# The output weight of an attention layer, split into halves earlier and kept in DRAM

## The chip, the cores and the metric

The kernel runs on one core of one Trainium2 chip. The core has a matrix engine (TensorE, PE in the profile; PEld is its weight load), three engines for element-wise work (VectorE, DVE; ScalarE, ACT; GpSimd, POOL) and SyncE (SP), which issues most of the DMA transfers. Each engine works through its own instructions in order and waits on semaphores for the others. The metric is the device time of one execution in microseconds. In the profile, TensorE's clock is the share of full speed that was granted to it.

## The reference, cut to what matters

One inference step of a small decoder: a Mamba-2 (SSD) layer, then a latent attention (MLA) layer, then a norm. There are two groups of tokens, a prompt of 1024 tokens and a sample of 8 sequences with 8 new tokens each and a paged cache of 2048 tokens. All is float32. Of the MLA layer this matters here:

```python
gate = proj[..., o3:]                                   # 1024 columns of w_in
s = (einsum('bqhc,bkc->bhqk', q_lat, ckv)               # 16 heads, latent of 256
     + einsum('bqhr,bkr->bhqk', q_pe, kpe)) * MLA_SCALE # rotary key of 32
p = exp(s - max(s)); acc = einsum('bhqk,bkc->bhqc', p, ckv); l = sum(p)
o = einsum('bhqc,chv->bqhv', acc / l, w_uv)
out = einsum('bte,ed->btd', o * silu(gate), w_out)      # w_out is 1024 x 1024
h = h + out                                             # then rms_norm(h, final_norm_w)
```

The sample's `ckv` and `kpe` come page by page from a pool through `page_table`, and partial results are merged with running maxima. The prompt is causal over itself.

## The kernel before

**Halves.** A matmul operand is kept as two rounded halves: `hi` is the value rounded to the matrix engine's input type and `lo` is the rest. A product is then three matmuls (hi x hi, hi x lo, lo x hi). `split` (lines 128 to 131) makes the halves: ScalarE copies `hi`, VectorE subtracts for `lo`. Every weight goes through a raw tile and a split before use (`load_w`, line 269 on).

**The stages of the MLA layer.** (1) `mla_in` (L1432): norm of the SSD layer's output, then eight gate blocks. `gate_block` (L1409) loads 128 columns of the gate's weight, splits them into tiles of tag `wg` (three buffers each for `hi` and `lo`), runs 72 matmuls (three groups of 24: 8 slices of the model dimension by three products), and ScalarE writes silu of each group into `gt`, which SP stores to DRAM (`g_d`). Between the blocks, `gather_kpe` (L1952) fetches the sample's rotary keys, transposes and splits them and stores the halves in DRAM (`kpe_d`). (2) The projections of keys, values and queries. (3) `mla_heads` (L1896): 16 heads of the prompt, 12 steps each. In a step `qk` (L1824) makes scores for 128 keys by 512 queries (`st`), ScalarE takes the exponential twice (`th` rounded, `P` full), POOL or VectorE subtracts for the rest `tl`, and three steps later (`LEAD`) `pv` (L1851) multiplies by the values. The row maxima come in as two further rows of the operand (rows 96 and 97): `maxpass` computes them one head ahead, and small DMAs (`kTh<-nr`, L1822) write them into the query operand. When a half of a head is done, its closing (L1881) multiplies by the softmax's denominator and the gate on POOL, and stores to DRAM (`og_d`). Key operands sit in four tiles `kT[0..3]`, query operands in three `qT`; head 15 takes `kT[0]` as its query tile (`q_of`, L1630). (4) The sample's pages: `flow` (L2225) runs over 32 items of 512 cached tokens. Item n's step transposes page n + 1 (`turn`, `ct` to `cTh`, `cTl`), transposes the weights of page n - 1 (`turn_p`, `pt`), makes scores (`scores`, tiles `sc4`, with the rotary key `tk` as the last product), takes the softmax (`weigh`, which gives `P`), fetches a later page, multiplies by the values of page n - 1 (`values`) and splits the raw page n + 1 (`halves`). Each sequence has four items; its new tokens add `first_scores`, `first_values` and `first_acc` at the first item, and `turn_acc` transposes the finished sum. The first eleven units of this flow (`FLOW`) run inside head 15. (5) `MlaOut.pieces` (L2327): for each of the 8 prompt tiles of 128 rows and the sample's rows, the gated output is read back from `og_d`, split into `oh`, `ol` and multiplied by the halves of the output weight `w5h`, `w5l`, in the order of `WORD`. `next(out.fill)` in the flow puts half of a tile's product into each page's step, from n = 4 on.

**The passage.** Between the last head's last product and the first pieces of the output (n = 2 to 5 of the flow) the tiles of the heads are freed and those of the output are opened over them.

**The weight before.** Two of eight raw slices of the output weight are loaded in `preload` at the beginning of head 15 (L2018), three more when the heads' tiles are free (L2274) and the last three as raw buffers get free (`weight`, L2309). `weight_split` (L2314) is called in the flow at n = 2 (four slices), 3 (two) and 4 (two): `hi` on ScalarE, `lo` in quarters on POOL for every second slice and on VectorE for the others.

**The rotary keys before.** `load_tk` (L2054) reads the halves of two pages, as plain numbers, into a staging tile `tkr` by three DMAs of 128 KB, and `round_tk` (L2061) copies each page on POOL into the operand `tk`.

**Who sets the order.** In the heads and the sample, TensorE's and GpSimd's instructions stay in the order in which the program writes them (`manual_schedule`). ScalarE, VectorE and SP are ordered by a planner that simulates a timeline; so their order can change where the program's text does not.

```python
            if len(closing) and closing[0][0] <= 12 * h + t:
                closing.pop(0)[1]()
            if len(held) > LEAD:
                c = hd.pv(*held.pop(0))
                if c:
                    closing.append((12 * h + t + 2, c))
```

## Time and profile before

| what | value |
|---|---|
| time, median of 3 | 1967.74 us (1966.07 to 1968.34) |
| the profiled execution | 1968.61 us, span 1966.8 us |
| TensorE busy | 1890.8 us, 96% |
| VectorE, ScalarE, GpSimd busy | 1185.9, 1108.1, 833.7 us |
| DMA moved | 207.02 MB, mean 105 GB/s |
| mean granted clock of TensorE | 0.984 |

The span runs from the first to the last instruction of the profiled execution; the time of that execution is 1.8 us longer. By the windows of the trace, the SSD layer lasts to about 1050 us of the span, the gates run from 1060 to 1168, the projections to 1340, the heads from 1340 to 1690, the passage from 1690 to 1734, pages and pieces to about 1930. A wait such as `PE pt L2174 <- ACT P L2089` reads: TensorE stood before the instruction of line 2174 that writes `pt`, and what ended the wait was ScalarE's instruction of line 2089 that writes `P`.

### The profile page before, as it was taken

What the parts mean: (1) busy time and instruction counts of PE and PEld (TensorE: products, weight loads), DVE (VectorE), ACT (ScalarE), POOL (GpSimd) and SP (SyncE); (2) the same over time, 40 slices, a digit from 0 to 9 for tenths busy, and PEclk for the clock granted to TensorE, in tenths of its full rate; (3) what the DMA queues carried; (4) which work ended last, traced back from release to release, by engine and by line L of the source; (5) the groups of instructions that cost most, each with busy time, mean ns of one, the idle gap of its engine ahead of it and who ended that gap; (6) DMA issues with size and microseconds to landing.
All of it is one profiled execution on the core that took longest, in us unless ns stands there. A gap on an engine that the chain in (4) does not pass through costs nothing.

```text
span 1966.8 us, 33784 instructions
## 1 busy us (share of the span) xinstructions
PE 1890.8 (96%) x11953; PEld 1735.2 (88%) x11953; DVE 1185.9 (60%) x2562; ACT 1108.1 (56%) x2605; POOL 833.7 (42%) x1138
## 2 busy tenths in 40 slices
PE   7999999999999999799999999999999999799998
PEld 6999999999999999687787998998888888678887
DVE  5457575757575757544425214566777776666665
ACT  5556666666666666653334324435777777655552
POOL 2037373737363657233000001104554556866661
PEclk9999999999999999899999999999999999899999
DMA  5213233333333332544544442222121113554451
GB/s 151 53 55 96 84 96 86 94 91 90 93 88 92 91 89 82 204 153 157 189 177 137 132 160 69 77 104 74 56 55 43 51 43 98 161 161 147 144 151 38
DMA packets 182545, 207.02 MB, mean 105 GB/s; under 512 B 19004, under 2 KB 147912, under 8 KB 181992
## 3 DMA queue, kind: packets, MB, share of 16 engines
q1 hardware_dynamic: 177544, 185.85, 31.2%
q0 software_dynamic: 4752, 18.88, 2.9%
q8 instruction: 95, 1.56, 0.3%
q14 instruction: 74, 0.61, 0.1%
q10 hardware_dynamic: 80, 0.13, 0.0%
HBM read 151.50 MB, written 53.15 MB: 104 GB/s over the span
## 4 chain that ended last, share of the span: by engine, by line
PE 77%; POOL 7%; issue 4%; DMA 4%; DVE 4%; ACT 3%; SPq 1%; POOLq 0%; DVEq 0%; ACTq 0%
PE pj L89 23%; PE pj L101 9%; PE pq L101 6%; PE pob L101 4%; PE poa L101 4%; POOL kvl L2147 3%; PE py L865 3%; PE sc L1801 2%; PE st L1834 2%; PE st L1835 2%; PE st L1836 2%; PE o L1867 2%; PE o L1866 1%; PE o L1865 1%; PE pk L101 1%
## 5 line engine op out<-in xcount | busy, mean ns | idle before, releaser
L89 PE MATMUL pj<-xh,wih 128*128 128x384 f32 (+1 forms) x768 | 255.7, 333 | 0.0
L89 PE MATMUL pj<-xh,wil 128*128 128x384 f32 (+1 forms) x768 | 251.2, 327 | 0.0
L89 PE MATMUL pj<-xl,wih 128*128 128x384 f32 (+1 forms) x768 | 251.0, 327 | 0.0
L1848 POOL TENSOR_TENSOR tl<-P,th 128x384 fp32r<-128x384 f32 (+1 forms) x144 | 132.9, 928 | 135.6 <-ACT P L1846 74.7
L131 DVE TENSOR_TENSOR wil<-wraw,wih 128x512 fp32r<-128x512 f32 x92 | 70.4, 765 | 173.8 <-ACT wih L130 173.8
L902 POOL TENSOR_TENSOR y<-y,xD 128x256 f32<-128x256 f32 x64 | 83.9, 1312 | 149.3 <-DVE y L901 138.5
L89 PEld LDWEIGHTS pj<-xh,wih 128*128 128x128 f32 x768 | 145.0, 189 | 0.2
L89 PEld LDWEIGHTS pj<-xl,wih 128*128 128x128 f32 x768 | 144.8, 189 | 0.3
L89 PEld LDWEIGHTS pj<-xh,wil 128*128 128x128 f32 x768 | 144.6, 188 | 0.0
L101 PE MATMUL pj<-wih,xh 128*128 128x256 f32 x504 | 143.3, 288 | 0.0
L101 PE MATMUL pj<-wil,xh 128*128 128x256 f32 (+1 forms) x504 | 139.2, 282 | 0.0
L1845 ACT ACTIVATE th<-st 128x512 fp32r<-128x512 f32 x192 | 94.4, 492 | 68.3 <-PE st L1841 46.6
L497 DVE SCALAR_TENSOR_TENSOR acc<-raw,vec,acc 128x1112 f32<-128x1112 f32 x84 | 130.5, 1554 | 0.2
L101 PE MATMUL pj<-wih,xl 128*128 128x256 f32 x448 | 126.6, 283 | 0.0
L2147 POOL TENSOR_TENSOR kvl<-pgr,kvh 128x256 fp32r<-128x256 f32 x128 | 98.7, 798 | 53.7 <-ACT kvh L2145 53.7
L131 POOL TENSOR_TENSOR xddl<-xdd,xddh 128x256 fp32r<-128x256 f32 x64 | 63.2, 987 | 119.5 <-ACT xddh L130 119.5
L130 ACT CAST Ch<-acc 128x128 fp32r<-128x128 f32 x56 | 16.9, 301 | 152.8 <-PE py L89 152.8
L101 PEld LDWEIGHTS pj<-wih,xh 128*128 128x128 f32 x504 | 96.0, 191 | 0.0
L1846 ACT ACTIVATE P<-st 128x512 f32<-128x512 f32 x192 | 93.4, 486 | 2.7 <-DVE tl L1848 2.1
L101 PEld LDWEIGHTS pj<-wil,xh 128*128 128x128 f32 (+1 forms) x504 | 93.0, 185 | 0.6
L840 ACT ACTIVATE M<-M,tok 128x128 f32<-128x128 f32 (+1 forms) x288 | 90.5, 388 | 1.8 <-DMA M<-acs_d 1.8
L101 PEld LDWEIGHTS pj<-wih,xl 128*128 128x128 f32 x448 | 85.5, 191 | 0.0
(981 smaller groups left out, 6276.0 us busy)
## 6 DMA issues: line engine op xcount, KB each, us to landing
wraw<-in_ssd_w_in SPq DMA_DIRECT2D x92, 256.0 KB
M<-acs_d SPq DMA_DIRECT2D x64, 256.0 KB
y_d<-xD SPq DMA_DIRECT2D x64, 128.0 KB
s<-in_state_ssm SPq DMA_DIRECT2D x32, 256.0 KB
out_s_ssm<-s SPq DMA_DIRECT2D x32, 256.0 KB
wraw<-in_ssd_w_out SPq DMA_DIRECT2D x16, 512.0 KB
q_d<-qt SPq DMA_DIRECT2D x32, 192.0 KB
qp<-q_d SPq DMA_DIRECT2D x8, 768.0 KB
```

Source lines behind the costliest of these rows:

```text
L89: nc.tensor.matmul(out, a, b, start=(i == 0), stop=(i == n - 1))
L101: nc.tensor.matmul(o, a, b, start=(j == 0), stop=(j == len(ops) - 1))
L131: (eng or nc.vector).tensor_tensor(lo, src, hi.bitcast(F32), op=ALU.subtract)
L497: nc.vector.scalar_tensor_tensor(acc, self.raw[bi][:, j : j + n], k.convw[j][:, blk : blk + 1], acc, op0=ALU.mult, op1=ALU.add)
L840: nc.scalar.activation(M[:m, h, :m], M[:m, h, :m], AF.Relu, bias=c.tk[:, 0, 4 * g + h : 4 * g + h + 1], scale=-1.0)
L865: nc.tensor.matmul(py[:m, h * 64 : h * 64 + 64], c.M[:m, h, :m], c.xdt[:m, h * 64 : h * 64 + 64], start=True, stop=True)
L902: nc.gpsimd.tensor_tensor(y[:m], y[:m], c.xD[:m], op=ALU.add)
L1801: nc.tensor.matmul(ps[:, :n], qh[:96, 128 * i : 128 * i + 128], kh[:96, 512 * c : 512 * c + n], start=True, stop=True)
L1845: nc.scalar.activation(th[:, :n], ps[:, :n], AF.Exp, scale=SCALE)
L1846: nc.scalar.activation(P[:, :n], ps[:, :n], AF.Exp, scale=SCALE)
L1848: eng.tensor_tensor(tl[:, :n], P[:, :n], th[:, :n].bitcast(F32), op=ALU.subtract)
L2147: nc.gpsimd.tensor_tensor(rl[:, r], raw[:, r], rh[:, r].bitcast(F32), op=ALU.subtract)
```

## The change

1. **The output weight is split in the gate stage.** After each gate block b = 2 to 7 one slice of the weight is loaded (512 KB), split into two tiles of the gates' tag `wg`, and both halves are stored to a DRAM tensor `w5_d`; two more follow the last block. `weight`, `weight_split`, `WSP` and `WENG` go.
2. **The halves are read back.** `preload` at head 15 reads three slices: `WORD[0]` into new tiles, the next two into the key tiles `kT[2]` and query tiles `qT[2]`, which nothing needs after head 14's last scores. For that the key and query tiles have 128 partitions in place of 98, and `kT[2]`, `qT[2]` are in a pool of their own (`kq3`) that stays open until the end. `WORD[3]` goes into `kT[0]` when `MlaOut` is made, after the heads. `WORD[4]` to `WORD[7]` go into new tiles, their loads called in the flow at n = 2 and n = 4.
3. **The rotary key halves** are read straight into the operand: one tile `tk` for two pages, six DMAs of 64 KB; `tkr` and the POOL copy go.
4. **Two moves.** `first_acc` is called at n = 1, 5, ... after `turn_p` in place of n = 0, 4, ... before `values`. The closing of a head's half is called three steps after its last product in place of two.
5. `late_open`, which makes the sample's last two tiles, is called at once.

The matrix engine has the same number of instructions after as before. On VectorE, two of the four copies of rotary rows at the start of the heads come ahead of the last `fold` of the queries.

```diff
...
 PRE = 4
 Q0 = 9
 OUT0 = (4, 5)
-WSP = (2, 2, 2, 2, 3, 3, 4, 4)
-WENG = (2, 0, 2, 0, 2, 0, 2, 0)
 WORD = (0, 4, 6, 1, 2, 3, 5, 7)
 NWA = 8
 NR0 = 13
...
     k.nc.sync.dma_start(k.g_d[b], gt)
 
 
+def out_weight_halves(k, wp, raws, kk):
+    nc = k.nc
+    raw = load_raw(raws, 8, 128).rearrange("p a e -> p (a e)")
+    nc.sync.dma_start(raw, k.I["mla_w_out"][0][kk * 128 : kk * 128 + 128])
+    hi, lo = (wp.tile([128, 8, 128], F32R, tag="wg" + x, name=f"wo{x}{kk}", bufs=3).rearrange("p a e -> p (a e)")
+              for x in "hl")
+    split(k, hi, lo, raw)
+    for j, t in enumerate((hi, lo)):
+        nc.sync.dma_start(k.w5_d[kk, j], t.bitcast(F32))
+
+
+def mla_gates(k, wp, raws):
+    for b in range(2, 8):
+        yield from gate_block(k, wp, raws, b)
+        out_weight_halves(k, wp, raws, WORD[b - 2])
+    for kk in WORD[6:]:
+        out_weight_halves(k, wp, raws, kk)
+
+
 def load_cw(k, pool, raws, c0, n, tag):
     wi = k.I["mla_w_in"][0]
     return [load_w(k, pool, wi[kk * 128 : kk * 128 + 128, c0 : c0 + n], 1, n, f"{tag}{kk}", 1, raws) for kk in range(8)]
...
+    k.w5_d = k.dram.tile([8, 2, 128, D], F32, name="w5_d")
...
         k.kvh = mp.tile([128, 2, SEQ], F32R, name="kvh")
         k.kvl = mp.tile([128, 2, SEQ], F32R, name="kvl")
         k.kvs = [k.cm.tile([128, 2, 64], F32R, name=f"kvs{x}") for x in "hl"]
-        gates = (None for b in range(2, 8) for _ in gate_block(k, wg, rw, b))
+        gates = mla_gates(k, wg, rw)
         with open_pool(tc, name="kg", bufs=1, side="right") as kg:
             gk = gather_kpe(k, kg)
             next(gk)
...
         self.maskr, self.maskt = mk[:, 0:512], mk[:, 512:640]
 
     def add_q(self, pool, j):
-        t = (pool.tile([98, SEQ], F32R, name=f"qTh{j}"), pool.tile([98, SEQ], F32R, name=f"qTl{j}"))
+        t = (pool.tile([128, SEQ], F32R, name=f"qTh{j}"), pool.tile([128, SEQ], F32R, name=f"qTl{j}"))
         self.k.nc.gpsimd.memset(t[1][96:98].bitcast(F32), 0.0)
         self.qT.append(t)
 
...
+    def open(self, st, right, psum):
         k, tc, nc, I = self.k, self.k.tc, self.k.nc, self.k.I
         self.psum = psum
+        top = right.enter_context(open_pool(tc, name="kq3", bufs=1, side="right"))
+        self.add_k(top, 2)
+        self.add_q(top, 2)
         sp = self.sp = st.enter_context(open_pool(tc, name="sp3", bufs=1, side="right"))
-        for j in range(2, NKT):
-            self.add_k(sp, j)
+        self.add_k(sp, 3)
         self.add_v(sp, 1)
         self.load_mask()
     def wt(self, name):
...
 
     def qk(self, h, qc, jb):
         k, nc, sp = self.k, self.k.nc, self.sp
-        qh, ql = self.q_of(h)
-        kh, kl = self.kT[h % NKT]
+        qh, ql, kh, kl = (x[:98] for x in (*self.q_of(h), *self.kT[h % NKT]))
         o = max(0, jb - 4 * qc) * 128
         n = 512 - o
         ks = slice(128 * jb, 128 * jb + 128)
...
             units[PF:PF] = [g] * 2
             units += [g] * 2
         if h + 1 == MH:
-            sm.preload()
+            sm.preload(st, hd)
             flow = sm.flow()
             units = [flow] * FLOW
         total, done = len(units), 0
...
             if len(held) > LEAD:
                 c = hd.pv(*held.pop(0))
                 if c:
-                    closing.append((12 * h + t + 2, c))
+                    closing.append((12 * h + t + 3, c))
     for x in held:
         c = hd.pv(*x)
         if c:
...
         k.kpe_d.append(d)
 
 
+def load_halves(k, w, kk):
+    for j, t in enumerate(w):
+        k.nc.sync.dma_start(t.bitcast(F32), k.w5_d[kk, j])
+
+
 class Sample:
     def __init__(self, k, pool):
         nc, I = k.nc, k.I
...
         tag, bufs = self.tags[tag]
         return self.psum.tile([128, 512], F32, tag=tag, name=name, bufs=bufs)
 
-    def preload(self):
+    def preload(self, st, hd):
         k = self.k
-        self.pre = ExitStack()
-        pp = self.pre.enter_context(open_pool(k.tc, name="pre4", bufs=1))
-        self.wraw = {}
-        for kk in WORD[:2]:
-            self.wraw[kk] = pp.tile([128, D], F32, name=f"w5p{kk}")
-            k.nc.sync.dma_start(self.wraw[kk], k.I["mla_w_out"][0][kk * 128 : kk * 128 + 128])
+        pp = st.enter_context(open_pool(k.tc, name="pre4", bufs=1))
+        self.w5 = dict(zip(WORD, ([pp.tile([128, D], F32R, name=f"w5p{x}") for x in "hl"], hd.kT[2], hd.qT[2], hd.kT[0])))
+        for kk in WORD[:3]:
+            load_halves(k, self.w5[kk], kk)
 
     def load_cn(self, b):
         self.cn = self.ep.tile([NT, KVL], F32, tag="cn", name=f"cn{b}", bufs=1)
...
         self.tags = {x: (x, SB[x]) for x in ("tr", "sc4", "on")}
 
     def late_open(self, st):
-        self.pre.close()
         ap = st.enter_context(open_pool(self.k.tc, name="ap4", bufs=1))
         self.accT = ap.tile([128, 2, NB, 128], F32, name="accT")
         self.gs = ap.tile([128, 8, 64], F32, name="gs4")
...
 
     def load_tk(self, n):
         k, nc = self.k, self.k.nc
-        self.tkr = self.ep.tile([96, 4, 256], F32, tag="tkr", name=f"tkr{n}", bufs=1)
+        t = self.ep.tile([96, 2, 4, 128], F32R, tag="tk", name=f"tk{n}", bufs=2)
         for j in range(3):
-            src = k.kpe_d[j % 2][:, :, 128 * n : 128 * n + 256].rearrange("r c x -> c r x")
-            nc.sync.dma_start(self.tkr[32 * j : 32 * j + 32], src)
-
-    def round_tk(self, n):
-        tk = self.ep.tile([96, 4, 128], F32R, tag="tk", name=f"tk{n}", bufs=2)
-        RT(self.k.nc)(tk, self.tkr[:, :, 128 * (n % 2) : 128 * (n % 2) + 128])
-        self.tk[n] = tk
+            for x in range(2):
+                src = k.kpe_d[j % 2][:, :, 128 * (n + x) : 128 * (n + x) + 128].rearrange("r c x -> c r x")
+                nc.sync.dma_start(t[32 * j : 32 * j + 32, x].bitcast(F32), src)
+        self.tk[n], self.tk[n + 1] = (t[:, x].rearrange("p r x -> p (r x)") for x in range(2))
 
     def load(self, n):
         k, nc = self.k, self.k.nc
...
         return gs
 
     def flow(self):
-        N = len(self.items)
+        k, N = self.k, len(self.items)
         for n in range(-1, N + 1):
             t, out = n + 1 < N, self.out
             if t:
...
                 yield
             if n > 0:
                 self.turn_p(n - 1)
+            if n % 4 == 1:
+                self.first_acc(n // 4)
             if t:
                 self.turn(n + 1, 1)
                 yield
...
                 self.load(n + PRE)
             if n == N - 2:
                 self.late_loads()
-            if t:
-                self.round_tk(n + 1)
             if n % 2 == 0 and n + 2 < N:
                 self.load_tk(n + 2)
+            if n in (2, 4):
+                for kk in WORD[n + 2 : n + 4]:
+                    load_halves(k, out.ws[kk], kk)
             if out and (n in OUT0 or max(OUT0) < n <= N - HOLD):
                 next(out.fill, None)
-            if out and n in WSP:
-                out.weight_split(WORD[WSP.index(n)])
-            if n % 4 == 0 and n < N:
-                self.first_acc(n // 4)
             if n > 0:
                 self.values(n - 1)
             if t:
                 self.halves(n + 1)
-            if out:
-                for x in range(1, WSP.count(n)):
-                    out.weight_split(WORD[WSP.index(n) + x])
-                if n + 1 == OUT0[0]:
-                    next(out.fill)
-                    self.k.nc.sync.dma_start(out.fw, self.k.I["final_norm_w"].partition_broadcast(128))
+            if out and n + 1 == OUT0[0]:
+                next(out.fill)
+                self.k.nc.sync.dma_start(out.fw, self.k.I["final_norm_w"].partition_broadcast(128))
             yield
 
 
 def mla_sample(k, sm, flow):
     with ExitStack() as st:
         psum = st.enter_context(open_pool(k.tc, name="ps4", bufs=1, space=PS))
-        out = MlaOut(k, st, psum)
+        sm.late_open(st)
+        out = MlaOut(k, st, psum, sm.w5)
         sm.open(st, psum, out)
-        out.raw = sm.wraw
-        for kk in WORD[2:5]:
-            out.weight(kk)
         out.fill = fill = out.pieces(range(8))
         next(fill)
-        for _ in flow:
-            if not hasattr(sm, "accT") and not any(kk in out.raw for kk in WORD[:2]):
-                sm.late_open(st)
+        drain(flow)
         last = None
         for x in TAIL:
             if x == "a":
...
 
 
 class MlaOut:
-    def __init__(self, k, st, psum):
+    def __init__(self, k, st, psum, w0):
         tc, nc, I = k.tc, k.nc, k.I
         self.k, self.psum = k, psum
         self.wp = st.enter_context(open_pool(tc, name="wp5", bufs=1, side="right"))
         sp = self.sp = st.enter_context(open_pool(tc, name="sp5", bufs=1, side="right"))
         self.fw = sp.tile([128, D], F32, name="fw")
...
+        self.ws = w0
+        for kk in WORD[4:]:
+            self.ws[kk] = [self.wp.tile([128, D], F32R, name=f"w5{x}{kk}", bufs=1) for x in "hl"]
+        load_halves(k, self.ws[WORD[3]], WORD[3])
 
     def pieces(self, tiles, src=None):
         k, nc, sp, ws = self.k, self.k.nc, self.sp, self.ws
```

More of the change, by code (lines that the diff above doesn't have):

```diff
@@ L1461, in mla_in @@
         kp = right.enter_context(open_pool(tc, name="kTp", bufs=1, side="right"))
-        k.kT = (kp.tile([98, SEQ], F32R, name="kTh0"), kp.tile([98, SEQ], F32R, name="kTl0"))
+        k.kT = (kp.tile([128, SEQ], F32R, name="kTh0"), kp.tile([128, SEQ], F32R, name="kTl0"))
         hp = mid.enter_context(open_pool(tc, name="hp", bufs=1, side="right"))
@@ L1641, in add_k @@
         nc, k = self.k.nc, self.k
-        t = (pool.tile([98, SEQ], F32R, name=f"kTh{j}"), pool.tile([98, SEQ], F32R, name=f"kTl{j}"))
+        t = (pool.tile([128, SEQ], F32R, name=f"kTh{j}"), pool.tile([128, SEQ], F32R, name=f"kTl{j}"))
         for a, b in zip(t, k.kT):
@@ L2305, in __init__ @@
         self.fw = sp.tile([128, D], F32, name="fw")
-        self.raw = {}
-        self.ws = [[self.wp.tile([128, D], F32R, name=f"w5{x}{kk}", bufs=1) for x in "hl"] for kk in range(8)]
-    def weight(self, kk):
-        k, nc, wp = self.k, self.k.nc, self.wp
-        self.raw[kk] = self.sp.tile([128, D], F32, tag="h5", name=f"w5r{kk}", bufs=3)
-        WQ(nc).dma_start(self.raw[kk], k.I["mla_w_out"][0][kk * 128 : kk * 128 + 128])
-    def weight_split(self, kk):
-        hi, lo = self.ws[kk]
-        raw = self.raw.pop(kk)
-        nc, x = self.k.nc, WENG[WORD.index(kk)]
-        if x & 1:
-            nc.gpsimd.tensor_copy(hi, raw)
-        else:
-            nc.scalar.copy(hi, raw)
-        for c in (slice(256 * j, 256 * j + 256) for j in range(4)) if x & 2 else (slice(0, D),):
-            (nc.gpsimd if x & 2 else nc.vector).tensor_tensor(lo[:, c], raw[:, c], hi[:, c].bitcast(F32), op=ALU.subtract)
-        if 2 <= WORD.index(kk) < 5:
-            self.weight(WORD[WORD.index(kk) + 3])
+        self.ws = w0
+        for kk in WORD[4:]:
+            self.ws[kk] = [self.wp.tile([128, D], F32R, name=f"w5{x}{kk}", bufs=1) for x in "hl"]
+        load_halves(k, self.ws[WORD[3]], WORD[3])
     def pieces(self, tiles, src=None):
@@ L2431, in layer_mla @@
         psum = heads.enter_context(open_pool(tc, name="ps3", bufs=1, space=PS))
-        hd.open(heads, psum)
+        hd.open(heads, right, psum)
         sm = Sample(k, qp)
@@ L2436, in layer_mla @@
         heads.close()
-        right.close()
         with tc.manual_schedule(engines={nc.tensor.engine, nc.gpsimd.engine}):
             mla_sample(k, sm, flow)
+        right.close()
         k.mps.close()
```

2 lines of the change are left out of this document (removed).

## The prediction

> **What bounds the kernel now.** I read the page's busy times and its chain first, then the windows from the last heads to the first pages, then the waits of PE there.
>
> ```profile
> PE 1890.8 (96%) x11953; PEld 1735.2 (88%) x11953; DVE 1185.9 (60%) x2562; ACT 1108.1 (56%) x2605; POOL 833.7 (42%) x1138
> PE 77%; POOL 7%; issue 4%; DMA 4%; DVE 4%; ACT 3%; SPq 1%; POOLq 0%; DVEq 0%; ACTq 0%
> ```
>
> PE is busy for 96% of the span of 1966.8 us and the change takes no matmul away, so time can only be won where PE idles (76 us in all) or runs slowly. The windows below hold, after the limits, the width, then the busy us of PE, PEld, DVE, ACT and POOL, then PE's granted clock, the DMA share and GB/s.
>
> ```profile
> 1650.00:1660.00 10.00, 6.65 (x23) 5.48 (x22) 4.55 (x6) 6.36 (x12) 7.19 (x6) 0.70 0.24 76
> 1660.00:1670.00 10.00, 10.00 (x66) 9.13 (x66) 4.59 (x13) 7.03 (x20) 7.13 (x10) 0.95 0.42 128
> 1670.00:1680.00 10.00, 8.29 (x39) 6.46 (x38) 5.36 (x8) 7.13 (x17) 9.17 (x10) 0.90 0.09 20
> 1680.00:1690.00 10.00, 10.00 (x62) 9.05 (x61) 5.16 (x9) 6.02 (x15) 8.06 (x11) 0.93 0.34 100
> 1690.00:1700.00 10.00, 9.22 (x65) 8.13 (x64) 6.54 (x16) 7.40 (x14) 5.96 (x8) 1.00 0.51 165
> 1700.00:1710.00 10.00, 5.67 (x28) 4.52 (x27) 8.07 (x12) 8.06 (x14) 10.00 (x11) 0.83 1.10 317
> 1710.00:1720.00 10.00, 6.98 (x18) 4.78 (x19) 7.58 (x6) 3.44 (x5) 9.56 (x13) 0.66 0.63 181
> 1720.00:1730.00 10.00, 6.36 (x36) 5.49 (x35) 8.65 (x10) 4.64 (x9) 8.63 (x11) 0.83 0.75 252
> 1730.00:1740.00 10.00, 10.00 (x60) 8.76 (x59) 5.34 (x13) 5.09 (x12) 5.13 (x7) 1.00 0.28 101
> ```
>
> PE idles 3.35, 1.71, 0.78, 4.33, 3.02 and 3.64 us here, 16.8 us in 80, and after most holes its clock is below 1.00. The wait list (1600 to 1967) names the holes:
>
> ```profile
> PE pt L2174 <- ACT P L2089: 6.2, 6, 3.4
> PE sc L89 <- POOL tk L2063: 4.0, 1, 4.0
> PE act L2205 <- ACT cTh L130: 3.6, 1, 3.6
> PE o L1867 <- POOL tl L1848: 3.4, 1, 3.4
> PE o40n L2125 <- ACT pn L2118: 1.7, 1, 1.7
> ```
>
> The timeline prices a slow stretch by the starts of equal matmuls:
>
> ```profile
> 1714.25 0.63 PE L101 MATMUL p<-w5l,oh 128*128 128x512 f32 x1
> 1714.68 0.63 PE L101 MATMUL p<-w5h,ol 128*128 128x512 f32 x1
> ...
> 1729.74 0.39 PE L101 MATMUL p<-w5l,oh 128*128 128x512 f32 x1
> 1729.97 0.40 PE L101 MATMUL p<-w5h,ol 128*128 128x512 f32 x1
> ```
>
> They are 0.43 us apart slow and 0.23 us fast, so slow time is 46% lost. The clock missing in the windows, (1 - clock) x 10 summed, is 3.5 us after the `tl` hole, 1.7 after `o40n`, and 1.7 + 3.4 + 1.7 = 6.8 in the passage (1690 to 1730). At half clock, twice that is slow time, of which 46% is lost: 3.2, 1.6 and 6.3 us. Hole and slow stretch together: `tl` 6.6, `o40n` 3.3, passage 11.0 + 6.3 = 17.3; in all 27 us.
>
> **The change, part by part. Work that goes.** Eight weight splits and 32 casts of keys leave the passage and the pages.
>
> ```profile
> L2321 ACT CAST w5h<-w5r 128x1024 fp32r<-128x1024 f32 x6 | 6.3, 1053 | 5.1 <-DMA w5r<-in_mla_w_out 5.1
> L2323 POOL TENSOR_TENSOR w5l<-w5r,w5h 128x256 fp32r<-128x256 f32 x12 | 9.4, 807 | 0.0
> L2323 POOL TENSOR_TENSOR w5l<-w5p,w5h 128x256 fp32r<-128x256 f32 x4 | 3.9, 994 | 2.6 <-ACT w5h L2321 2.6
> L2063 POOL CAST tk<-tkr 96x512 fp32r<-96x512 f32 x8 | 5.0, 626 | 1.8 <-DMA tkr<-kpe_dh 1.7
> ```
>
> POOL loses 9.4 + 3.9 + 5.0 us between 1640 and 1740, where its slices are 86 to 100% busy. The `tk` wait (3.97 us) ends on a cast that stood in POOL's queue behind `w5l`; the key now lands in the operand by DMA (six of 64 KB instead of three of 128 KB), so this hole goes: 4.0. The `act` wait (3.64 us) ends on `cTh`, which ACT did late: between 1640 and 1740 its queue stood 5.1 us on the DMAs of raw weights, all in the passage; that DMA wait is gone: 3.6.
>
> **What stays in the passage.** `pt` of page 3 waits for `P` and `P` stands on ACT behind `oh`, which waits for the gated output to come back from DRAM. Both still hold.
>
> ```profile
> 1690.04 0.27 PE L1867 MATMUL o<-tl,Vh 128*128 128x128 f32 x1
> ...
> 1704.97 0.86 PE L2174 MATMUL pt<-ident,P 128*128 128x128 f32 x4 [3.37 <-ACT P L2089]
> ...
> 1695.17 0.45 SPq L1882 DMA_DIRECT2D og_d<-og  x1
> ...
> 1697.32 0.59 SPq L2337 DMA_DIRECT2D og<-og_d  x1
> ...
> 1711.58 0.38 SPq L2337 DMA_DIRECT2D og<-og_d  x1
> ...
> 1706.86 1.05 ACT L130 CAST oh<-og 128x1024 fp32r<-128x1024 f32 x1 [0.82 <-issue]
> ...
> 1716.82 1.05 ACT L130 CAST oh<-og 128x1024 fp32r<-128x1024 f32 x1 [0.68 <-DMA og<-og_d]
> ```
>
> From the last `o` matmul the store starts 5.1 us later and the reload 7.3. The second reload was issued at 1711.6 and ended a wait of 0.68 of ACT at 1716.8; I count 4.6 to 5.2 for it, so `og` is there at +11.9 to +12.5 and `oh` ends at +13.0 to +13.6. Then `P41n`, `kvh`, `cTh` and `P` follow on ACT (some 0.3 + 1.05 + 0.6 + 0.7), so `P` at +15.7 to +16.3. Before, PE reached `pt` at 1704.97 - 3.37 = 1701.6 (+11.5) and waited 3.4; now 4.2 to 4.8; I take 4.5 (bounds 3.4, as before, and 5.6). It costs a slow stretch too, 2.2 us, the mean of the three (6.3 / 3). Passage: 17.3 - 4.5 - 2.2 = 10.6 gained; I take 9.7, leaving 0.9 for small waits. Bounds: 5 (a second hole like `act` stays with its clock) and 13 (only 4.3 of idle left).
>
> **The `tl` and `o40n` holes (heads 14, 15).** The closing of a head's half goes one step later, so POOL does `tl` before the multiply `og` that waits:
>
> ```profile
> 1652.32 1.27 POOL L1881 TENSOR_TENSOR og<-og,rl 64x512 f32<-64x512 f32 x1 [4.47 <-DVE og L1877]
> 1653.67 3.73 POOL L1848 TENSOR_TENSOR tl<-P,th 128x512 fp32r<-128x512 f32 x3
> ```
>
> One of the three `tl`s (1.24) now comes first, two stay behind `og`. PE's wait shrinks by 1.3 at least; I take a rest of 1.5 with a shorter slow stretch, 4.0 of 6.6 won (bounds 1.3 and 6.6). `first_acc` moves from before the values of a page to the next step, a page's worth of PE work after ACT's copy `pn`, so `o40n` finds it done: 1.7 + 1.6 = 3.3, taken whole (bounds 1.7 and 3.9, if the clock had lost more). At the start of the heads PE waits for `mx`, which stands on DVE behind four copies of the rotary rows:
>
> ```profile
> PE sc L1801 <- DVE mx L1806: 2.9, 1, 2.9
> ```
>
> Two of the four move ahead of an earlier fold, where DVE idles for half a microsecond: 0.5 (0 to 1).
>
> [...]
>
> **Work that is added at the gates.** Eight loads of 512 KB, eight ACT copies, eight DVE subtracts, 16 stores of 512 KB (12.6 MB) in about 75 us, on SP's queue between the gates' loads.
>
> ```profile
> L131 DVE TENSOR_TENSOR wgl<-wraw,wgh 128x1024 fp32r<-128x1024 f32 x5 | 6.1, 1226 | 27.7 <-ACT wgh L130 27.6
> L130 ACT CAST wgh<-wraw 128x1024 fp32r<-128x1024 f32 x5 | 5.3, 1051 | 8.6 <-PE pj L89 8.6
> ...
> 1110.00:1120.00 10.00, 10.00 (x64) 9.97 (x63) 0.00 (x0) 1.80 (x3) 0.00 (x0) 1.00 0.27 74
> ...
> 1140.00:1150.00 10.00, 10.00 (x64) 10.00 (x63) 0.00 (x0) 1.42 (x3) 0.99 (x2) 1.00 0.97 387
> ```
>
> 8 x 1.05 = 8.4 us on ACT and 8 x 1.23 = 9.8 on DVE, in 75 us; in the slices shown ACT is busy for 1.4 to 1.8 of 10 and DVE for none. The DMA adds 168 GB/s, to 74 in the first slice; the one with the rotary keys' stores (387) has no room, but there the last gates' weights are already in. But the halves share the three buffers of the gates' weights: ACT's next `wgh` waits until the stores of an older half are done, and ACT's queue holds the evacuation of a gate behind it. At 64 matmuls in 10 us a gate block of 72 lasts 11.3. The buffer that gate b + 2 takes was last used by the half split a block earlier: cast, subtract and stores (1.05 + 1.23 + 4 to 5, near the 4.6 of a 512 KB reload above) fill 6.3 to 7.3 of it, and the cast itself may wait up to 3 us for its load: 1 to 2 us are left where it is tightest. I take 0; bounds 0 and -5 (two holes like `o40n`).
>
> **Added before head 15.** SP issues 2 MB of halves into `kT[2]`, `qT[2]` when head 14's last `st` has read them, just ahead of the small DMA `kTh<-nr` with the row maxima of head 15.
>
> ```profile
> 1663.49 1.26 SPq L1822 DMA_DIRECT2D kTh<-nr  x2
> ...
> 1668.04 0.40 PE L1834 MATMUL st<-kTh,kTh 98*128 98x512 f32 x1
> ```
>
> The rows were needed 4.5 us after the issue. Four issues of 0.5 us delay it by 2, and 2 MB at the 387 GB/s of the full slice above last 5.4. If the small DMA waits for all of it, it is late by some 3 us, and with a slow stretch 6; if it passes, by 0 to 1. I take -3.0 (0 to -6). [...] No row of before shows a small DMA behind 2 MB.
>
> The other halves, 4 x 1 MB, are needed at page 5's piece, some 29 us after the last `o`; SP issues the last of them after `og`, and they land at about +25 by the rate above. Their cover is that margin of 4 us: if the stall at page 3 were gone, they would be late by 1 to 2.
>
> **The sum.** Passage 9.7 + `tl` 4.0 + `o40n` 3.3 + heads' start 0.5 - rows 3.0 - gates 0 = 14.5 us. The profiled execution has 1968.6 us (span 1966.8), 0.9 above the median of 1967.7; 14.5 less is 1954 against the profiled execution, 1953 against the median. I forecast 1953.
>
> **Rivals.**
> 1. Transfers are late. The rows wait fully (-6), `tl` gains 1.3, the passage gives 5: 5 + 1.3 + 3.3 - 6 = 3.6, so 1964; with a passage of 8, 1961. For it speaks the DMA share of 1.10 at 1700 and that 5 MB of halves are read there where 3 MB of raw weights were; against it that four of the five are needed only at page 5. Chance 0.16.
> 2. Slower: the gates starve. If the stores of a half take over 2 us longer than these 5, the copies `wgh` and with them the evacuations behind them on ACT come late in each later block; PE, with nothing else to do there, stands 2 to 3 us and then runs slowly for 1.5. Five such blocks are 20 us, against 14.5 won: about 1973. What speaks for it: one queue of SP carries all, in order, and a store waits at its head for the split. Against: the DMA share of 0.27 in the first slice. It decides from three late blocks on. Chance 0.20.
> 3. No change to be measured: rows -6, gates -4, passage 5, the rest 5.6: 1967. Measured differences under 0.2% (3.9 us) can't be told from none here. Chance 0.09.
> 4. Everything goes: `og` lands before ACT needs it, the rows pass the bulk. 13 + 6.6 + 3.9 + 0.5 = 24: 1944. The late halves speak against it. Chance 0.07.
>
> **How the numbers follow.** The forecast has 0.48. Faster by over 0.2%: 0.48 + 0.16 + 0.07 = 0.71; within: 0.09; slower: 0.20. The range goes from rival 4 to a little above no change, 1943 to 1969, and leaves out most of rival 2. The forecast's own range is 1946 to 1960.
>
> **What would show it.** PE's waits after: `sc` for `tk` and `act` for `cTh` gone; `pt` for `P` still there with 3.4 to 5.6 us; `o` for `tl` under 2; a new `st` wait for the rows of head 15 of 0 to 4 us. Between 1090 and 1170 PE must show 10.00 in each slice at clock 1.00; a row of 8 or 9 there is rival 2. ACT waits for DMA of a weight's half in the passage would be rival 1. I am wrong if PE loses at the gates, or if the passage keeps two holes.

## The result and the profile after

| kernel | median, us | lowest to highest | ratio to before, 95% |
|---|---|---|---|
| before, 10 executions | 1967.9 | 1966.07 to 1970.69 | |
| changed, 10 executions | 1972.4 | 1969.44 to 1974.99 | 1.0023 [1.0013, 1.0033] |

The change costs 4.5 us. A gain of 14.5 was forecast, with a range of 1943 to 1969: the forecast is wrong in sign. The profiled execution of the changed kernel took 1970.4 us (span 1968.6), 2 us less than its median, so the traces show 1.8 us of the loss.

The wait list of PE, changed kernel (engine, line, instruction, what ended the wait: us in total, times, longest):

```profile
PE pt L2191 <- ACT P L2106: 11.1, 8, 5.5
...
PE o L1885 <- POOL tl L1866: 5.9, 1, 5.9
PE act L2222 <- ACT ac L2144: 3.4, 7, 0.5
...
PE st L1852 <- DMA kTh<-nr: 3.2, 1, 3.2
```

Set beside the list before: `sc <- tk` (4.0), `act <- cTh` (3.6) and `o40n <- pn` (1.7) are gone. `tl` has grown from 3.4 to 5.9, the long `pt` wait from 3.4 to 5.5, the rows of head 15 are late by 3.2, a wait of `act` stands in each of seven sequences (0.43 to 0.50 us) where before there was only the one of 3.6, and in the pages there are six short `pt` waits of 0.85 to 0.88 us in place of four of 0.54.

The windows of the changed kernel, in the columns of those before (busy PE first, then behind POOL the clock, the DMA share, GB/s):

```profile
1650.00:1660.00 10.00, 4.09 (x18) 3.37 (x17) 3.47 (x5) 4.41 (x8) 4.62 (x4) 0.83 0.39 99
1660.00:1670.00 10.00, 9.62 (x55) 8.38 (x54) 5.26 (x12) 6.04 (x17) 7.31 (x10) 0.83 0.69 250
1670.00:1680.00 10.00, 7.15 (x30) 6.16 (x31) 1.99 (x3) 4.57 (x10) 4.46 (x6) 0.83 0.24 93
...
1700.00:1710.00 10.00, 4.54 (x33) 3.99 (x32) 5.33 (x13) 5.27 (x12) 6.57 (x10) 0.89 0.86 307
1710.00:1720.00 10.00, 10.00 (x49) 8.46 (x49) 4.16 (x10) 3.11 (x8) 2.41 (x3) 0.77 1.06 379
1720.00:1730.00 10.00, 9.57 (x56) 8.04 (x56) 6.29 (x13) 6.00 (x13) 4.70 (x6) 1.00 1.07 348
...
1770.00:1800.00 30.00, 28.64 (x156) 24.04 (x155) 18.66 (x42) 14.54 (x33) 15.52 (x20) 0.94 0.43 133
1800.00:1830.00 30.00, 28.66 (x175) 24.65 (x174) 19.20 (x42) 16.11 (x34) 15.63 (x20) 1.00 0.49 149
```

The passage has two quiet windows fewer (1710 to 1730 was 6.98 and 6.36). The last heads (1650 to 1680) have more idle time. The pages are new as a place of loss: 1.35 us idle in 30. The kernel before had 29.46 there:

```profile
1770.00:1800.00 30.00, 29.46 (x180) 25.45 (x179) 19.67 (x43) 16.89 (x37) 19.27 (x25) 1.00 0.50 151
```

The eight copies of `accT`, one per sequence, mark the pages' length. First the kernel before, then the changed one (first and last start):

```profile
L2206 DVE COPY accT<-act x8: 418/425/426, 1727.1 to 1942.6; 128x256 f32<-128x256 f32 x8
```

```profile
L2223 DVE COPY accT<-act x8: 420/425/425, 1722.1 to 1944.3; 128x256 f32<-128x256 f32 x8
```

At the first mark the changed kernel is 5.0 us ahead, at the last 1.7 behind. So the pages last 222.2 us in place of 215.5 and lose 6.7; the forecast had nothing there.

The same PE instructions in both traces show where the time went. The changed kernel is 0.8 us ahead at the beginning of the last two heads (`nkp` at 1638.18, before 1638.99) and 3.1 behind at the last `o` of the heads (1693.14, before 1690.04). So the last two heads lose 3.9 us, the stretch from there to the first mark wins 8.1, and the pages lose 6.7.

### The profile page after: what moved, and what is told of

The parts are those of the page before. It is cut to its first block, busy times and chain, and to the rows that moved or that the text cites. A ratio compares the mean times of both kernels' runs of the same rounds, so it can differ in the third digit from the quotient of the medians.

```text
span 1968.6 us, 33836 instructions
## 1 busy us (share of the span) xinstructions
PE 1889.0 (96%) x11953; PEld 1734.6 (88%) x11953; DVE 1170.0 (59%) x2566; ACT 1106.9 (56%) x2605; POOL 790.7 (40%) x1090
## 4 chain that ended last, share of the span: by engine, by line
PE 79%; issue 6%; POOL 5%; DMA 3%; DVE 3%; ACT 2%; SPq 0%; POOLq 0%; DVEq 0%; ACTq 0%
PE pj L87 24%; PE pj L99 9%; PE pq L99 5%; PE poa L99 4%; PE pob L99 4%; POOL kvl L2164 4%; PE py L863 3%; PE sc L1820 2%; PE st L1852 2%; PE pz L99 2%; PE st L1853 2%; PE o L1885 2%; PE st L1854 2%; PE o L1884 1%; PE o L1883 1%
```

## The experiments

All are timed in five rounds beside the kernel before, whose median was 1968.0 to 1968.4 in them. Two theories stand against each other at the start: the calls that were moved (`first_acc`, the closing) cost the time, or the DMA traffic that was moved does.

### One part of the change undone

**`first_acc` back at its old place.**

```diff
-            if n % 4 == 1:
-                self.first_acc(n // 4)
...
+            if n % 4 == 0 and n < N:
+                self.first_acc(n // 4)
             if n > 0:
                 self.values(n - 1)
```

> The changed kernel with first_acc called at its old place (n = 0, 4, ... before values). Theory A (the move of first_acc costs the pages: each sequence of four pages takes 32.2 us after against 31.3 before, the waits act <- ac of 0.5 and pt <- P of 0.87 in place of 0.54): both waits go back, seven sequences gain 6 us, the o40n hole of 1.7 us with its slow stretch comes back (about 3), so some 3 us faster than the changed kernel, 1969 us. Rival B (the pages are slower because of the rotary keys' six small DMAs or the halves' traffic): the period of 32.2 us stays, and with the o40n hole the time is about 1975.

Measured: 1963.5 us, ratio 0.9973 [0.9964, 0.9982]. 8.9 us less than the changed kernel, three times what was expected; both waits are gone from the pages, which last 212.0 us.

**The halves for `kT[2]`, `qT[2]` behind the row maxima.** A one-element write on POOL, whose instructions stay in the program's order, holds the loads back: the first of them goes out at 1674.1, in the changed kernel at 1662.0.

```diff
+            if h + 1 == MH and t == 5:
+                sm.load_late()
...
-        for kk in WORD[:3]:
+        for kk in [0]:
+            load_halves(k, self.w5[kk], kk)
+
+    def load_late(self):
+        k = self.k
+        for kk in [4, 6]:
+            for x in self.w5[kk]:
+                k.nc.gpsimd.memset(x[0:1, 0:1].bitcast(F32), 0.0)
             load_halves(k, self.w5[kk], kk)
```

> The changed kernel with the four loads of halves into kT[2] and qT[2] issued after step 5 of head 15 (a one-element POOL write into each tile holds them back), so behind the small DMA with head 15's row maxima. Theory A (the 3.2 us wait of st for kTh<-nr is the small DMA standing behind 2 MB): the wait is below 0.3 us and the slow stretch behind it goes, 3 to 5 us less than the changed kernel, about 1968. Rival B (the row maxima are late because VectorE writes nr late after the tl hole): the wait stays above 2 us and the time does not change.

Measured: 1964.9 us, 0.9981 [0.9972, 0.9990], 7.5 less than the changed kernel. Here is SP's queue of the changed kernel (start, duration):

```profile
1662.03 0.35 SPq L2007 DMA_DIRECT2D kTh<-w_d  x1
...
1664.92 1.31 SPq L1841 DMA_DIRECT2D kTh<-nr  x2
```

and what PE did for it:

```profile
1672.85 0.47 PE L1852 MATMUL st<-kTh,kTh 98*128 98x512 f32 x1 [3.23 <-DMA kTh<-nr]
```

4 KB issued by 1666.2 were there at 1672.8, 6.6 us later, behind four loads of 512 KB. With the loads behind it, the small DMA goes out at nearly the same time (1664.49) and PE has no wait:

```profile
1664.49 1.29 SPq L1841 DMA_DIRECT2D kTh<-nr  x2
```

The wait and its slow stretch are 3.2 + 1.6 us by the trace; the median says 7.5, and by the two intervals that difference is uncertain by some 2.5. So the cause of the wait is shown, and its price lies between 5 and 10 us by the medians.

**The first slice held back too.** The same edit, with `[0, 4, 6]` in the late list and nothing early.

> As the run before, with the two loads of the first slice (w5ph, w5pl) held back as well. Theory A (the tl hole of 5.9 us comes from the gathers of the first two pages, which take 8.1 us to land behind 1 MB of halves and the rotary keys, against 5.3 before; og on POOL and kvh on ACT wait for them): the gathers land in about 5 us, the hole shrinks to 2 to 3.4 us, and the time is another 3 to 5 us less than with the rows first alone, about 1964. Rival B (the later closing puts og in front of three tl in a worse order): the hole stays at 5 to 6 us.

Measured: 1965.4 us, 0.9982 [0.9970, 0.9993]: no better than the run before. Theory A is half right: the gathers of the first two pages land in 6 us and the hole of 5.6 us at `tl` becomes two of 2.1 and 0.2 (`st` for `P`, `o` for `tl`). But the time stays. PE's busy time from 1680 to 1690 is 8.03 here and 10.00 in the run before. The trace shows why: the loads that were moved go out just ahead of a later gather (issued at 1679.4), which lands in 8.3 us where those of the run before land in 6.0 at most, POOL's closing multiply `og` waits for that one, two `tl` stand behind `og`, and `o` waits for `tl` again, now at another place:

```profile
1687.95 1.26 POOL L1899 TENSOR_TENSOR og<-og,rl 64x512 f32<-64x512 f32 x1 [3.25 <-DMA pgr<-in_cache_ckv,ptidx]
```

```profile
1690.07 0.39 PE L1885 MATMUL o<-tl,Vh 128*128 128x256 f32 x1 [2.04 <-POOL tl L1866]
```

The landing of the first two gathers (least, median, most, us) in the kernel before, in the changed one, and here:

```profile
DMA to landing us min/median/max: 4.4/4.8/5.3
```

```profile
DMA to landing us min/median/max: 9.2/9.2/9.2
```

```profile
DMA to landing us min/median/max: 5.9/6.0/6.2
```

**The closing two steps after the last product, as before.**

```diff
-                    closing.append((12 * h + t + 3, c))
+                    closing.append((12 * h + t + 2, c))
```

> The changed kernel with the closing two steps after the last product, as before. Theory A (the tl hole comes from the gathers' landing): the hole stays between 5 and 6.5 us and the time within 2 us of the changed kernel's 1972.4. Rival B (the later closing makes the hole longer): the hole goes back to about 3.4 us, and the time to about 1968.

Measured: 1975.4 us, 1.0030 [1.0019, 1.0042]. The hole stays at 5.5 us: the place of the closing does not make it. (The median is 3 us above that of the changed kernel, but the two intervals overlap. Its `pt` hole is 6.8 in the trace, and its pages last 227.4 us, since the clock falls behind four of the six pairs of `pt` and `act` waits, one of them with a `pt` wait of 1.8, where it does so behind one pair in the changed kernel.)

```profile
L2223 DVE COPY accT<-act x8: 417/424/425, 1724.6 to 1952.0; 128x256 f32<-128x256 f32 x8
```

What does make the hole is seen in the list of those that waited for the gathers; in this run:

```profile
  POOL og L1899: 6.7, 1
```

`og`, the closing multiply, reads no page. But it waits for the gathers that were issued ahead of it on POOL, and everything behind it on POOL, `tl` too, waits along. In the changed kernel the timeline names another releaser:

```profile
1655.30 1.27 POOL L1899 TENSOR_TENSOR og<-og,rl 64x512 f32<-64x512 f32 x1 [6.98 <-ACT th L1863]
```

Its own inputs do not explain these 7 us: the last `og` of VectorE before it ended at 1649.4 and the last `rl` of ScalarE at 1650.4. The second gather, issued at 1645.9, landed 9.2 us later, at 1655.1. Why `og` carries this wait, and the `tl` that stands between the gathers and `og` does not, no run shows.

### Parts of the change alone, on the kernel before

**Only `first_acc` moved.** The edit of the change, in the kernel before.

> The kernel before with nothing but first_acc moved to n = 1, 5, ... Theory A (the move costs by itself): act <- ac of 0.5 us and pt <- P of 0.87 us appear in seven sequences, 6 us lost and up to 3 by clock, the o40n hole gained (1.7 to 3.3): slower by 3 to 6 us, 1971 to 1974. Rival B (the move costs only with the rest of the change, where og and the halves load the queues): within 2 us of before, or faster by 3.

Measured: 1987.2 us, 1.0093 [1.0072, 1.0114], 19 us slower: Theory A has the sign and the two waits right, and a third or less of the cost. The first `act` alone waits 7.5 us there (3.6 before). In each of the six later sequences PE shows two holes and then the slow clock (0.94 to 0.96 in the windows of 30 and 40 us that hold it), and the pages last 233.5 us in place of 215.5:

```profile
1759.25 0.66 PE L2174 MATMUL pt<-ident,P 128*128 128x128 f32 x4 [1.36 <-ACT P L2089]
...
1761.61 0.56 PE L2205 MATMUL act<-ident,ac 128*128 128x128 f32 x2 [0.50 <-ACT ac L2127]
...
1763.25 0.63 PE L89 MATMUL sc<-cTh,qlh 128*128 128x512 f32 x1
1763.68 0.63 PE L89 MATMUL sc<-cTl,qlh 128*128 128x512 f32 x1
...
1765.54 0.40 PE L101 MATMUL p<-w5h,ol 128*128 128x512 f32 x1
1765.78 0.40 PE L101 MATMUL p<-w5h,oh 128*128 128x512 f32 x1
```

The reason for the first hole stands in the order: `o42n`, the product of `first_acc`, takes 0.6 us, and before it stood between the scores of a page and the transpose `pt` of its weights. PE's cover for the softmax became 0.6 us shorter. The second: `act` uses the same PSUM tag as `ct`, `pt` and `o4n`, which has four buffers. With `first_acc` in the same step it is the fifth tile of the step and needs the buffer of the first, which VectorE's `cTl` frees last. In the changed kernel `cTl` runs from 1753.14 to 1753.83 and `act` starts at 1753.92:

```profile
1753.14 0.69 DVE L129 TENSOR_TENSOR cTl<-ct,cTh 128x512 fp32r<-128x512 f32 x1 [1.20 <-ACT cTh L128]
```

```profile
1751.56 0.66 PE L2191 MATMUL pt<-ident,P 128*128 128x128 f32 x4 [0.88 <-ACT P L2106]
1752.14 0.69 PE L2142 MATMUL o42n<-cn,pn 8*128 8x256 f32 x2
1752.77 0.66 PE L2152 MATMUL ct<-ident,pgr 128*128 128x128 f32 x4
1753.92 0.44 PE L2222 MATMUL act<-ident,ac 128*128 128x128 f32 x2 [0.50 <-ACT ac L2144]
```

(The list names `ac` as the releaser; it ended at 1753.87, at nearly the same moment. That the buffer is the cause of the second hole is read from the code and these times; no run separates the two.)

**Only the rotary keys read straight into the operand.** `load_tk` as in the change, `round_tk` and its call gone.

> The kernel before with nothing but the rotary keys read straight into the operand. Theory A (of the passage only the sc <- tk hole of 4.0 us hangs on the cast): that hole goes with its slow stretch, 3 to 6 us faster, 1963 to 1965; the pages do not change since TensorE has no wait for tk there. Rival B (the six small DMAs for page 2 and 3 go out early and load the queue ahead of the first gathers): the tl hole grows from 3.4 to 5 us or more and eats the gain, 1967 to 1969.

Measured: 1963.9 us, 0.9982 [0.9972, 0.9993], 4.5 faster. Both theories were half right. The hole `sc <- tk` goes, and the one at `tl` grows to 5.7, with the gathers landing in 7.4 us:

```profile
PE o L1867 <- POOL tl L1848: 5.7, 1, 5.7
PE pt L2171 <- ACT P L2086: 4.8, 2, 4.4
```

So the small transfers of the keys, which now go out early, are enough to delay the gathers; the halves of the weight are not needed for it. And the four `pt` waits of 0.54 us in the pages are gone, which nobody had expected; by the marks the pages last 214.2 us, 1.3 less than before, since another wait (`o42n`) grew by 0.9. In the kernel before, VectorE's tiny `mn` (one number per partition) lasts 0.56 us at the first page of five sequences, while POOL copies `tk`:

```profile
1786.73 1.37 POOL L2063 CAST tk<-tkr 96x512 fp32r<-96x512 f32 x1
```

```profile
1787.57 0.56 DVE L2083 TENSOR_TENSOR mn<-mx,mx43n 128x1 f32<-128x1 f32 x1
```

Without the copy the same instruction takes 0.15:

```profile
1784.68 0.15 DVE L2080 TENSOR_TENSOR mn<-mx,mx43n 128x1 f32<-128x1 f32 x1
```

So beside the copy `mn` takes 0.56 us, and without it 0.15; what slows it down, no run shows. `mn` is in the chain from the scores to `P`, so PE's waits of 0.54 us for `P` go with it.

**Only the splits and stores in the gate stage.** The kernel before, with `mla_gates` and `out_weight_halves` of the change added; the halves in DRAM are not read.

> The kernel before with the output weight's halves made and stored in the gate stage as in the change, and never read; the rest uses its own weight splits as before. Theory A (the gate stage hides all of it): TensorE's windows from 1090 to 1170 stay at 10.00 and the time within 2 us of before, 1968.4. Rival B (the stores hold back the gates' evacuation or the loads behind them): 3 us or more slower.

Measured: 1967.9 us, 0.9999 [0.9990, 1.0008]. TensorE stays full through the busiest DMA time of the stage:

```profile
1110.00:1120.00 10.00, 10.00 (x64) 9.93 (x63) 3.13 (x4) 4.62 (x7) 0.00 (x0) 1.00 0.81 268
...
1140.00:1150.00 10.00, 10.00 (x63) 10.00 (x62) 1.23 (x1) 2.37 (x4) 0.00 (x0) 1.00 0.99 409
```

### What is left, taken away step by step

**Both first corrections together**, `first_acc` back and the row maxima ahead of the halves.

> The changed kernel with first_acc at its old place and the halves for kT[2], qT[2] issued behind the row maxima. The two alone gave 8.9 and 7.5 us. Theory A (they are separate losses): they add up, 1972.4 - 16.4 = 1956 us; of the changed kernel's holes tl (5.6), o40n (1.7) and pt <- P (5.5) are left. [...]

Measured: 1958.6 us, 0.9944 [0.9927, 0.9962], 13.8 less than the changed kernel. They add up to within 2.6 us. The pages' marks:

```profile
L2232 DVE COPY accT<-act x8: 418/425/426, 1721.6 to 1933.9; 128x256 f32<-128x256 f32 x8
```

212.3 us, 3.2 less than before and 9.9 less than in the changed kernel. Of the 3.2, the four waits for `P` are 2.2, less 0.4 for a longer wait of `o42n`. Most of the rest is a slow stretch of the kernel before: behind its `act` hole the scores start 0.43 us apart until 1728.9, in place of 0.23, which costs some 1.1 us behind the first mark.

**`oh` held back behind page 4's split.**

```diff
+                self.k.nc.gpsimd.memset(out.oh0[0:1, 0, 0:1].bitcast(F32), 0.0)
                 next(out.fill)
...
+            if i == 0:
+                self.oh0 = oh
```

> As e5, with the split of the first gated output (oh) on ScalarE held back behind the split of page 4 by a one-element POOL write, so that P of page 3 goes ahead of it. Theory A (the pt hole of 5.1 to 6.8 us is P standing behind oh, which waits for the reload of og): the hole goes to at most 1 us and the slow stretch behind it too, 5 to 8 us less than e5, about 1949; a wait of PE for a half of the weight or for oh at the first piece may take 1 to 2 of it. Rival B (POOL's and ScalarE's queues are late there anyway): a hole of 4 us or more comes back at the next page, and the time is within 2 us of e5.

Measured: 1959.4 us, 0.9954 [0.9935, 0.9972], no gain. The hole of 6.7 us at `pt` became 1.9, 0.4 (for `oh`), 1.3 (for `ol`) and, 28 us on, 1.9 with a slow stretch. With `P` ahead of `oh` on ScalarE no time is won: the gated output comes late, and PE stands for it at one place or another.

**The closings of heads 13 to 15 on VectorE.** This is done on top of both corrections. It takes the multiply away from the engine whose queue carries the gathers.

```diff
-            nc.gpsimd.tensor_tensor(og[pj], og[pj], rl[pj], op=ALU.mult)
+            (nc.vector if h >= 13 else nc.gpsimd).tensor_tensor(og[pj], og[pj], rl[pj], op=ALU.mult)
```

> As e5 (first_acc back, halves behind the row maxima), and the closing multiplies of heads 13 to 15 on VectorE instead of POOL. Theory A (POOL's og carries the wait for the gathers issued ahead of it, and tl on POOL and the store of the gated output stand behind it; that makes the tl hole of 5.2 us and, by the late reload, the pt hole of 6.7 us): the tl hole falls below 3 us (ScalarE still waits some 3 us for the gather at kvh), the pt hole to 2 to 4 us; 5 to 9 us less than e5's 1958.6, about 1952. Rival B (the holes hang on ScalarE's queue alone: kvh <- pgr and oh <- og): both stay within 1 us of e5's, and the time too.

Measured: 1950.3 us, 0.9906 [0.9890, 0.9923]; 8.3 less than the run with both corrections, with intervals that do not overlap, and the lowest median of this study. Its longest waits of PE are

```profile
PE o L87 <- DVE pTl L129: 3.0, 3, 1.1
PE pt L2200 <- ACT P L2115: 1.9, 2, 1.4
PE o40n L2151 <- ACT pn L2144: 1.7, 1, 1.7
```

The hole at `tl` is gone altogether. At `pt` 1.4 us are left of 6.7; new small waits stand in part in its place, 0.7 us for `pTh` and three for `pTl`. Both holes had one cause, the closing on POOL. In the changed kernel the last closing stood on POOL behind a gather; then came the reload, `oh` and `P`:

```profile
1698.95 1.28 POOL L1899 TENSOR_TENSOR og<-og,rl 64x512 f32<-64x512 f32 x1 [2.58 <-DMA pgr<-in_cache_ckv,ptidx]
```

```profile
1706.23 1.04 ACT L128 CAST oh<-og 128x1024 fp32r<-128x1024 f32 x1 [4.62 <-DMA og<-og_d]
```

**The way free for the first gathers as well.** The first slice is held back until after step 5 of head 15, and the keys of pages 2 and 3 until POOL comes to their place in the flow, on top of the edit before.

> As e9, with the first slice's halves and the rotary keys of pages 2 and 3 also held back until after step 5 of head 15, so that no bulk stands ahead of the first two gathers. Theory A (gathers land late behind the bulk): they land in 5 to 6 us, ScalarE's wait at kvh is below 1 us, the tl hole below 1 us; 2 to 5 us less than e9. Rival B (the bulk only moves on to the next gathers or to the reload of og, as it did between e2 and e3, where a hole of 5.6 went and no time was won): the pt hole grows by what the tl hole loses, time as e9.

Measured: 1954.5 us, 0.9926 [0.9912, 0.9940]. The gathers land in 5.0 us, and nothing is won by it: the median is 4 us above that of the run before, with intervals that overlap. Theory A is out, since the `tl` hole that it was to shorten had gone with the closings already. Rival B has the time right and not the reason: the `pt` hole is 1.4 as before, and the wait for `pTh` ahead of it is 1.7 in place of 0.7. Whether the bulk does harm in the passage is open.

**`first_acc` moved for the first sequence alone**, on top of that.

> As e10, with first_acc moved for the first sequence alone (n = 1), the others at the old place. Theory A: the o40n hole of 1.7 us goes and nothing comes, since the act <- ac and pt <- P waits of the move arise only where the output's pieces run: 1.5 to 3 us less than e10. Rival B (in the heads too the move takes PE's cover from the wait for P): no gain.

Measured: 1951.6 us, 0.9906 [0.9890, 0.9921], 2.9 less by the medians, again with intervals that overlap. The hole at `o40n` goes and nothing comes in the pages (212.2 us by the marks). But a hole at `pt` of 5.5 us is back in its trace. In the run before, PE had waited 1.7, 0.9 and 1.4 us (`pTh`, `pTl`, `pt`) on the same stretch; here it comes to `pt` without the first two, and `P` still stands behind the reload:

```profile
1696.85 1.04 ACT L128 CAST oh<-og 128x1024 fp32r<-128x1024 f32 x1 [4.68 <-DMA og<-og_d]
```

No harm of the move is seen where it runs inside the heads; the harm is in the later sequences, where the output's pieces run. With the other holes gone, this trace has the way of the gated output to DRAM and back at the end of the passage.

## Why the prediction was wrong, point by point

- **The passage (forecast +9.7).** From the last `o` of the heads to the first `act` the traces have 1690.04 to 1726.3 before and 1693.1 to 1721.7 after: 7.7 us won. The holes `tk` and `act` went as forecast. The `pt` hole was taken at 4.5 (3.4 to 5.6) and measured 5.5; the mechanism was right, the way of the gated output was mis-sized. The store was copied from before as 5.1 us after the last `o`, and came 7.1 after it (1700.25), because POOL's closing waited 2.6 us for a gather. The reload went out right behind it, at +7.7 in place of +7.3, and `oh` began at +13.1, where the forecast had the reload there by +12.5 at the latest. (The forecast read POOL's slices from 1640 to 1740 as 86 to 100% busy; its own rows have this from 1670 to 1680 and from 1700 to 1730, and 51 to 81% in the others. No term hangs on it.)
- **`tl` (forecast +4.0).** Wrong step: "POOL does `tl` before the multiply `og` that waits" was to shorten the wait. The hole grew by 2.5 us. The row quoted there, `og` idle for 4.47, names VectorE's `og` as the releaser; but the second gather, issued at 1646.7, landed 5.3 us later, at 1652.0, just before `og` began, and that was not considered. In the changed kernel the gathers landed in 9.2 us in place of 4.8, behind keys and halves, and two runs (the closing back; the closing on VectorE) show that the wait for them sits on `og`: the place of the closing hardly matters, its engine does.
- **`o40n` (forecast +3.3).** Wrong step, and the largest: "`first_acc` moves from before the values of a page to the next step, a page's worth of PE work after ACT's copy `pn`, so `o40n` finds it done", taken whole. That `o40n` finds it done came true. But the step considered the one sequence in the wait list and not at the other seven calls, and put the move's cost at nothing. It was paid with 9.9 us in the pages, and undoing it alone gave back 8.9.
- **The rows (forecast -3.0, bounds 0 and -6).** The mechanism was right and the wait 3.2; with the slow stretch 4.8 by the trace, 7.5 by the run, so the worse end of the bounds was nearer than the 3.0. The trace has 6.6 us from the issue of 4 KB behind 2 MB to their use; for a small DMA that waits for all of the bulk the forecast had -6, 3 us worse than the middle, which it took.
- **The gates (forecast 0).** Right: 0.9999 alone. Rival 2 named this stage for a loss, so the one slower case was at the wrong place; that its 1973 is near the measured 1972.4 is luck, since PE is at 10.00 with clock 1.00 in every slice from 1090 to 1170.
- **The heads' start (forecast +0.5).** Waits of 2.9 + 1.5 became 1.5 + 1.1 + 1.2, 0.6 less. But the granted clock is lower behind them (0.63 and 0.86 between 1340 and 1360, before 0.84 and 0.81), and nothing is won: from a `pq` of the projections (1307.42 before, 1306.77 after) to the first `nmp` of the heads (1412.50, 1411.97) PE takes 105.1 us before and 105.2 after.
- **The pages (forecast 0).** They held terms that the sum did not have: -9.9 for `first_acc`, and +3.2 of which some 2 are the copies of `tk`, which had been counted as work off the path, and most of the rest the slow stretch behind the `act` hole, which the forecast had counted in the passage.

The terms by the two traces: +7.7 passage, -2.5 `tl`, +1.7 `o40n`, -3.2 rows, +0.6 start (its waits alone), -6.7 pages, together -2.4 without the slow stretches outside passage and pages; the traces differ by -1.8.

## What to carry to other kernels

An instruction that moves takes its own duration out of the cover of whatever wait it stood in front of, here the 0.6 us of `o42n` in front of `pt`: before a call in a loop is moved, count its duration as PE's cover at each of the places it leaves, and the tiles of its tag at each of the places it enters. In this kernel the gathers issued on POOL put their wait on a later POOL instruction that reads nothing of them (7.0 and 2.6 us in the changed kernel), so small work that the matrix engine waits for is better placed on another engine than the one which issues the gathers. Bulk loads are to be ordered behind the last small DMA that the matrix engine waits for (4 KB behind 2 MB were there after 6.6 us here, and PE stood 3.2 for them), and not merely as early as their destination is free.

## What was not expected of the hardware

Two short holes can cost the clock: 1.36 and 0.50 us within 3.7 were followed by 3.5 us at half rate (scores 0.43 us apart in place of 0.23) in the kernel with only `first_acc` moved (1761.8 to 1765.3), while in the kernel with the closings on VectorE the hole of 1.71 at `o40n` (1671.8) costs clock and the one of 1.42 at `pt` (1701.1) does not (0.83 and 1.00 in their windows):

```profile
1670.00:1680.00 10.00, 8.29 (x40) 6.90 (x39) 4.33 (x8) 6.86 (x17) 6.59 (x7) 0.83 0.74 272
...
1700.00:1710.00 10.00, 8.88 (x53) 7.35 (x54) 4.62 (x11) 5.24 (x13) 3.86 (x5) 1.00 1.03 410
```

The length of the holes does not decide alone: the pair of some 0.86 and 0.50 us that the moved `first_acc` makes is followed by a slow stretch in one of six sequences of the changed kernel's trace, and behind three of five such pairs (0.84 to 0.98 and 0.50) in that with the closing two steps after the last product.

This also accounts for the 8.9 us that undoing the move of `first_acc` gave. In the pages of the changed kernel its twelve waits sum to 8.2 us, the one slow stretch (0.94 in a window of 30 us) adds some 1.7 by the price of the forecast, and of these waits none is left when the move is undone; against it stand the `o40n` hole, which comes back with 1.7, and one new wait of 0.5. Together that is 7.7, and the difference of the medians is uncertain by 2 to 3.

And profiled executions differ by up to 5 us ahead of the edit (the first gather goes out at 1644.4 in the changed kernel's and at 1649.4 in that with `first_acc` put back), so stages are to be compared by their own marks, and kernels by their medians.
